# The streams' attention steps start five chunks later, the memory keys get a pool of their own, and a PSUM pair is allocated first

## The chip, the cores and the metric

One core of a Trainium2 chip runs the kernel. The metric is the device time of one execution in microseconds (us): 1756.99 as the median of three runs (1756.55 to 1760.46). TensorE is called PE below, VectorE DVE, ScalarE ACT, GpSimd POOL; SP is the engine that issues most loads, in order.

## The reference

One layer of an encoder step, for 1024 prompt frames and for 8 running streams of 16 frames each (1152 rows of 1024 values in all), in float32:

```python
h = _rmsnorm(x, ln_mix); u, va, q, k, vb = split(h @ w_in)
a_out = u * (tril(w_s) @ va_c + b_s)                    # spatial gating, chunks of 128
z = (q @ k.T) * 64 ** -0.5                              # 8 heads of 64
log_keep = where(mask, log_sigmoid(-z), 0)
between = cumsum(log_keep, reverse=True) - log_keep
sb_out = where(mask, exp(log_sigmoid(z) + between), 0) @ v
x = x + concat(_rmsnorm(a_out), _rmsnorm(sb_out)) @ w_out
s = (h2 @ w_mq) @ mk.T / 16; x = x + (softmax(s) @ mv) @ w_mo   # 4 heads of 256, 256 memory rows
x = x + (silu(h3 @ w_gate) * (h3 @ w_up)) @ w_down      # width 2816
```

The prompt attends to its own keys; a stream attends to its cached 256 keys and its own 16. For the prompt the memory keys and values are computed from mem_prompt, for the streams they are read from a cache.

## The kernel before

Every float32 product is done as three matmuls of a split operand: `split` (L126, L127) writes the rounded value on ACT and the remainder on DVE, `mm3` (L130 to L132) multiplies. The kernel runs in stages: A, the input projection and spatial gating; B, stick-breaking attention; C, the merge into the residual; D, memory attention; E, output projection and feed-forward; then the down projection and the last norm. The order of instructions on each engine is not that of the code: the framework's scheduler lays it down when the program is built, and the engines then run their own lists in order. A buffer that is used again is waited for by address.

**Stage B.** Each of the 8 heads has 12 chunks (`chunk`), 96 in all. A chunk computes z on PE (L385), two sigmoids on ACT (L411, L398), a running product on DVE (pr, L403), a product on POOL (beta, L405), transposes on PE (L389), a split into ath and atl, and products with the values into av. The tasks are started one per step; `tasks()` counts chunks in `n` and starts stream `b` (`stream`) when `n == S0 + SP * b`, with `SP = 10`, and after the eight streams `stream_tails`. A stream transposes its cached keys (kT, L503), and later sums into oTs (L538, and L557 in the tails). In each step, PE work from `memory()` (the memory keys and values of the prompt, weights called mw) and `merge_a()` (the spatial part of the merge) fills up to `SLOT`. At the end oT_d, the attention output in DRAM, is complete; stage C loads it as `or` (L764).

**Stage D.** For each of four heads, `prompt_head` and `stream_head` run side by side. `stream_head` loads cached keys in four pairs (L858), transposes and splits them (`keys`, tiles kth, ktl), multiplies (L934), takes a softmax, loads the cached values in four pairs (vh, vl, L951), and ends with four transposes (L959), a copy to ot (L961) and a store (L962). Buffers come from stack-like pools; stage D's are, in order, `d_q`, `d_k`, `d_a`, `e_z`, `e_k` (the streams' raw pairs, keys and values) and `e_a` (their softmax and results). Worked out from the tile shapes they reach to 67,584 bytes a partition before `e_k`, to 92,160 with it and to 99,328 with `e_a`.

**Stage E.** After `stL.close()` the next pools lie at the same addresses: `f_h` with ten slots of 9,216 bytes (0 to 92,160), then `f_g` with the gain gffn (to 96,256), then `f_x` with the residual tiles xt, three buffers of 4,096 bytes, of which the first ends at 100,352. `out_in(i)` loads xt (L1029) and the attention output or; `out_mm(i)` multiplies and adds on DVE (L1048). Tile 0 uses two accumulators (acc0) that stage D began; the other tiles use PSUM pairs, two of the eight banks each, which get banks in the order of their first use. `norm` (L148, L141, L142, L150) and `turn_halves` (transposes at L1060) follow.

Of the kernel before, what the change touches and what calls it, by code (L numbers as in the profile page):

```python
# [37 lines left out]
def stream_step(ctx: ExitStack, tc: tile.TileContext, I, O, cst):  # L38
    nc = tc.nc

    def pool(stack, name, bufs=1, **kw):
        return stack.enter_context(tc.tile_pool(name=name, bufs=bufs, reuse_waits="tile", **kw))
# [10 lines left out]
    def nm(s):  # L53
        uid[0] += 1
        return f"{s}_{uid[0]}"
# [5 lines left out]
    def ps(tag, shape):  # L61
        n = next(cur[tag])
        return psum[0].tile(shape, F32, tag=f"bank{n}", name=nm(tag))
# [57 lines left out]
    def split(hi, lo, src, gain=None):  # L121
        if gain is not None:
            nc.scalar.activation(hi, src, AF.Copy, scale=gain)
            nc.vector.scalar_tensor_tensor(out=lo, in0=src, scalar=gain, in1=hi.bitcast(F32), op0=ALU.mult, op1=ALU.subtract)
            return
        nc.scalar.copy(hi, src)  # L126
        nc.vector.tensor_tensor(out=lo, in0=src, in1=hi.bitcast(F32), op=ALU.subtract)  # L127
# [80 lines left out]
    with ExitStack() as st:  # L208
# [47 lines left out]
        for i in range(NT):  # L256
# [11 lines left out]
            kt = [ap.tile([P, 4, P], F32R, tag=f"kt{n}", name=nm("kt")) for n in range(2)]  # L268
# [100 lines left out]
    with ExitStack() as st:  # L369
# [44 lines left out]
        def pair(h, c, got):  # L414

            sh = {}
            spans = [(512, 2 * c), (0, 2 * c)] if c >= 2 else [(0, 2 * c)]
            for part, (s, _) in enumerate(spans):
                for qb in (2 * c, 2 * c + 1):
                    e = (qb + 1) * P if part == 0 else 512  # L420
                    yield chunk(h, c, qb, s, e, part, len(spans) - 1, sh, got)
# [62 lines left out]
        def stream_in(b):  # L484
            if b == B:
                vn = kp.tile([P, 2, 512], F32, tag="vr", name="vn")[:, 0]
                nc.sync.dma_start(vn, v_s)
                return vn
            kr = kp.tile([P, 2, 512], F32, tag="kr", name=nm("kr"))
            nc.sync.dma_start(kr, csk[b].rearrange("(n p) d -> p n d", p=P))  # L490
            vr = kp.tile([P, 2, 512], F32, tag="vr", name=nm("vr"))
            nc.sync.dma_start(vr, csv[b].rearrange("(n p) d -> p n d", p=P))
            return kr, vr
# [46 lines left out]
        def stream_tails(vn):  # L540

            tr = ps("tr", [P, P])
            tp_(tr, tails.rearrange("p b k -> p (b k)"), ident)
            wt = kp.tile([P, 4, PAST + Q], F32, tag="kT", name="wt")[:, :, 0:PAST].rearrange("p c (b w) -> p c b w", b=B)
            for c in range(4):
                nc.vector.tensor_tensor(out=wt[:, c], in0=tr[:, None, c * 32:(c + 1) * 32].broadcast_to([P, B, 2 * Q]),
                                        in1=own[:, :, None].broadcast_to([P, B, 2 * Q]), op=ALU.mult)
            yield
            yield
            for c in range(4):  # L550
                av = ps("tr", [P, B, 2, Q])
                mm(av.rearrange("p b e q -> p (b e q)"), lhsT=vn[:, c * P:(c + 1) * P], rhs=wt[:, c].rearrange("p b w -> p (b w)"),
                   start=True, stop=True)
                for e in range(2):
                    r = slice(e * 64, e * 64 + 64)
                    o = oTs[r, c].rearrange("p (b q) -> p b q", b=B)
                    nc.vector.tensor_tensor(out=o, in0=av[r, :, e], in1=o, op=ALU.add)  # L557
                yield
            nc.sync.dma_start(oT_d[:, NP:TOK].rearrange("(c p) t -> p c t", p=P), oTs)
# [131 lines left out]
                if i + 2 < NT:  # L691
                    ins.append(load(i + 2))

        S0 = 4
        SLOT = 4700
        ZC = 1
        LAG = 2
# [2 lines left out]
        def tasks():  # L700
            sgot[0] = stream_in(0)
            n, b = 0, 0
            for h in range(8):
                if 0 < h < 7:
                    head_in(h + 1)
                for c in range(4):
                    for g in pair(h, c, got):
                        yield g
                        n += 1
                        if n == S0 + SP * b and b <= B:  # L710
                            yield stream(b, sgot) if b < B else stream_tails(sgot[B])
                            b += 1
                        elif b and n == S0 + SP * (b - 1) + LAG + 6 and b <= B:
                            sgot[b] = stream_in(b)
# [32 lines left out]
    with stD:  # L747
# [56 lines left out]
        stL = ctx.enter_context(ExitStack())  # L804
# [3 lines left out]
        zp = pool(stL, "e_z")  # L808
        sk = pool(stL, "e_k", bufs=2)
        sa = pool(stL, "e_a")  # L810
        W = 144
        qm = zp.tile([P, 2, 2, 4 * W], F32R, name="qm")
        pm = zp.tile([P, 2, 2, 4 * W], F32R, name="pm")
        for t in (qm, pm):
# [17 lines left out]
        def split_blocks(t, j, src):  # L832
            v = t[:, j].rearrange("p g (b w) -> p g b w", w=W)
            split(v[:, :, :, 0:Q], v[:, :, :, 64:64 + Q], src.rearrange("p (g b q) -> p g b q", g=2, b=4))

        def flat(t):
            return t.rearrange("p n k -> p (n k)")

        def keys(pl, kr):
            tr = ps("tr", [P, 2, 2, P])  # L840
            for dc in range(2):
                for n in range(2):
                    nc.tensor.transpose(tr[:, dc, n, :], kr[:, n, dc * P:(dc + 1) * P], ident)
            kth = pl.tile([P, 2, 2, P], F32R, tag="kth", name=nm("kth"))
            ktl = pl.tile([P, 2, 2, P], F32R, tag="ktl", name=nm("ktl"))
            split(kth, ktl, tr)
            return kth, ktl
# [7 lines left out]
        def pairs(src, cs):  # L855
            for b in range(0, B, 2):
                r = sk.tile([P, 2, 2, 256], F32, tag="raw", name=nm("raw"))
                nc.sync.dma_start(r, src[b:b + 2, :, cs].rearrange("b (n p) d -> p b n d", p=P))  # L858
                yield b, r[:, 0]
                yield b + 1, r[:, 1]  # L860
# [63 lines left out]
        def stream_head(h, qr):  # L924
            cs = slice(h * 256, (h + 1) * 256)
            for dc in range(2):
                split_blocks(qm, dc, qr[dc][:, NP:TOK])
            ss = ps("ss", [P, 2, 256])
            for b, kr in pairs(cmk, cs):
                kt = keys(sk, kr)  # L930
                g, b4 = divmod(b, 4)
                for dc in range(2):
                    for n in range(2):
                        nc.tensor.matmul(ss[:, g], lhsT=qm[:, dc, g, b4 * P:(b4 + 1) * P], rhs=flat(kt[n][:, dc]),  # L934
                                         start=b4 == 0 and dc == 0 and n == 0, stop=b4 == 3 and dc == 1 and n == 1)
                if b % 4 == 3:
                    yield
            p = softmax(sa, fold(ss, "s"), 64)
            tr = ps("tr", [P, 2, P])
            for n in range(2):  # L940
                for g in range(2):
                    nc.tensor.transpose(tr[:, n, g * 64:(g + 1) * 64], p[lo_, g, n * P:(n + 1) * P], ident[lo_, lo_])
            for n in range(2):
                split_blocks(pm, n, tr[:, n])
            ov = ps("ov", [P, 2, 256])
            for b, vr in pairs(cmv, cs):
                vv = values(sk, vr)
                g, b4 = divmod(b, 4)
                for n in range(2):
                    for m in range(2):  # L950
                        nc.tensor.matmul(ov[:, g], lhsT=pm[:, n, g, b4 * P:(b4 + 1) * P], rhs=vv[m][:, n],  # L951
                                         start=b4 == 0 and n == 0 and m == 0, stop=b4 == 3 and n == 1 and m == 1)
                if b % 4 == 3:
                    yield
            oe = fold(ov, "s")
            tr = ps("tr", [P, 2, P])
            for dc in range(2):
                for g in range(2):
                    nc.tensor.transpose(tr[:, dc, g * 64:(g + 1) * 64], oe[lo_, g, dc * P:(dc + 1) * P], ident[lo_, lo_])  # L959
            ot = sa.tile([P, 2, P], F32, tag="ot", name=nm("ot"))  # L960
            nc.vector.tensor_copy(ot, tr)  # L961
            nc.sync.dma_start(omT_d[4][cs, :].rearrange("(c p) t -> p c t", p=P), ot)  # L962
# [43 lines left out]
    with ExitStack() as stE:  # L1006
# [6 lines left out]
        def slot(shape, name):  # L1013
            return slots.tile(shape, F32R, tag="h", name=name)

        def pair(n):
            return psum[0].tile([P, 2, 512], F32, tag=f"pair{n}", name=nm("pp"))

        b11, b21, b22 = ([slot([P, 4, TH], f"{t}{n}") for n in range(2)] for t in ("b11", "b21", "b22"))
        t1, t2, t3, t4 = (slots.tile([P, 4, TH], F32, tag="h", name=f"t{n}") for n in range(1, 5))  # L1020
        gffn = bcast(pool(stN, "f_g"), I["ln_ffn"].rearrange("l d -> (l d)"), D, "gffn")
# [376 lines left out]
```

## Time and profile before

| what | value |
|---|---|
| median of three runs | 1756.99 us |
| profiled execution, its own time | 1759.56 us |
| its span | 1757.8 us |
| PE busy | 1687.9 us, 96% of the span |
| DVE, ACT, POOL busy | 986.7, 676.2, 430.3 us |
| mean granted PE clock | 0.988 of full speed |
| DMA | 229.51 MB, mean 131 GB/s |

The shares are means over stages with different limits. An engine's idle time counts only where the others wait for it. The profile gives the granted clock as a share of 2.4 GHz; 0.50 is 1.2 GHz. In the profile's rows a start is counted from the span's start, and the bracket at the end of a row is the idle time ahead of it with what ended it.

### The profile page before, as it was taken

How to read it: one execution, taken by the hardware profiler on the slowest of the kernel's cores; microseconds unless marked ns; L12 is line 12 of the kernel's file. 1: busy time of each engine (PE TensorE's matmuls, PEld its weight loads, DVE VectorE, ACT ScalarE, POOL GpSimd, SP SyncE). 2: the span in 40 equal slices, each digit the busy share in tenths (PEclk: the TensorE clock that was granted, in tenths of full speed). 3: DMA queues.
4: the chain of work that ended last, by engine and by line, in shares of the span. 5: the costliest groups of instructions: out<-in, count | busy, mean ns of one | idle time of the engine just before them, and what ended most of it. 6: DMA issues, size and time to landing. Idle time of an engine off the chain costs nothing. (4 is left out here: it accounts for less than half of the span.)

```text
span 1757.8 us, 26293 instructions
## 1 busy us (share of the span) xinstructions
PE 1687.9 (96%) x10039; PEld 1498.9 (85%) x10039; DVE 986.7 (56%) x1481; ACT 676.2 (38%) x1326; POOL 430.3 (24%) x574
## 2 busy tenths in 40 slices
PE   8999998999999899999699999999999999999997
PEld 6889887777777799998577899999999999888886
DVE  5312345889788746545535866555555556444444
ACT  5322224777565436545422423233322333011123
POOL 2101224444343220000011254443443332000002
PEclk9999999999999999999899999999999999999999
DMA  8548235667644624343734122222222227322202
GB/s 272 164 165 267 78 114 172 184 193 227 209 135 133 191 99 139 111 131 110 234 127 122 67 81 88 76 76 76 76 76 76 75 89 247 130 102 102 102 13 96
DMA packets 178254, 229.51 MB, mean 131 GB/s; under 512 B 12177, under 2 KB 125457, under 8 KB 178129
## 3 DMA queue, kind: packets, MB, share of 16 engines
q1 hardware_dynamic: 146432, 163.46, 30.8%
q10 hardware_dynamic: 23504, 35.79, 5.5%
q0 software_dynamic: 8192, 28.58, 4.3%
q8 instruction: 80, 1.31, 0.3%
q14 instruction: 46, 0.37, 0.1%
HBM read 163.43 MB, written 64.36 MB: 130 GB/s over the span
## 5 line engine op out<-in xcount | busy, mean ns | idle before, releaser
L1203 PE MATMUL pp<-b,wg 128*128 128x288 f32 x1584 | 221.4, 296 | 3.5 <-ACT wg L126 2.4
L1203 PEld LDWEIGHTS pp<-b,wg 128*128 128x128 f32 x1584 | 213.5, 188 | 4.4 <-ACT wg L126 2.6
L131 PE MATMUL tr<-wd,hid 128*128 128x512 f32 x396 | 154.6, 391 | 0.0
L132 PE MATMUL tr<-wd,hid 128*128 128x512 f32 x396 | 154.0, 389 | 0.0
L130 PE MATMUL tr<-wd,hid 128*128 128x512 f32 x396 | 151.4, 389 | 0.0
L127 DVE TENSOR_TENSOR wg<-s,wg 128x512 fp32r<-128x512 f32 x88 | 86.9, 989 | 99.0 <-ACT wg L126 85.9
L1339 DVE TENSOR_TENSOR xr<-tr,xr 128x512 f32<-128x512 f32 x108 | 73.2, 688 | 119.9 <-PE tr L132 119.5
L405 POOL TENSOR_TENSOR beta<-beta,pr 128x512 f32<-128x512 f32 (+4 forms) x104 | 95.3, 918 | 144.3 <-DVE pr L403 125.5
L130 PE MATMUL acc<-wh,hah 128*128 128x512 f32 x288 | 114.6, 398 | 0.0
L132 PE MATMUL acc<-wh,hal 128*128 128x512 f32 x288 | 113.5, 394 | 0.0
L131 PE MATMUL acc<-wl,hah 128*128 128x512 f32 x288 | 113.2, 393 | 0.0
L126 ACT CAST hid<-hr 128x576 fp32r<-128x576 f32 x44 | 27.5, 670 | 190.5 <-PE tr L132 176.4
L131 PEld LDWEIGHTS tr<-wd,hid 128*128 128x128 f32 x396 | 74.3, 188 | 16.8 <-DVE wd L127 1.5
L126 ACT CAST wg<-s 128x512 fp32r<-128x512 f32 x88 | 54.2, 619 | 87.9 <-DVE g L1187 44.3
L130 PEld LDWEIGHTS tr<-wd,hid 128*128 128x128 f32 x396 | 74.3, 188 | 15.9
L132 PEld LDWEIGHTS tr<-wd,hid 128*128 128x128 f32 x396 | 74.3, 188 | 15.2
L126 ACT CAST wg<-raw 128x512 fp32r<-128x512 f32 x66 | 40.5, 622 | 118.2 <-PE pp L1203 46.7
L1049 POOL DMA_DIRECT2D x_d<-xt x9 | 5.6, 624 | 320.6 <-DVE xt L1048 320.6
L127 DVE TENSOR_TENSOR wl<-raw,wh 128x1024 fp32r<-128x1024 f32 x36 | 44.6, 1247 | 48.9 <-ACT wh L126 48.0
L1351 POOL TENSOR_SCALAR sm<-sm 128x1 f32<-128x1 f32 x9 | 7.1, 792 | 252.8 <-ACT junk L1344 252.8
L1115 POOL TENSOR_TENSOR s<-raw 128x512 f32<-128x512 f32 x22 | 28.9, 1313 | 158.5 <-DMA raw<-in_w_ffn_up_dram 77.8
L130 PE MATMUL acc<-hdh,wh 128*128 128x384 f32 x192 | 66.3, 345 | 0.0
(294 smaller groups left out, 4535.5 us busy)
## 6 DMA issues: line engine op xcount, KB each, us to landing
hr<-hid_d SPq DMA_DIRECT2D x44, 288.0 KB, 5.0
raw<-in_w_ffn_up_dram SPq DMA_DIRECT2D x24, 512.0 KB, 4.1
hid_d<-g ACTq DMA_DIRECT2D x42, 288.0 KB, 2.1
raw<-in_w_ffn_gate_dram SPq DMA_DIRECT2D x23, 512.0 KB, 3.9
raw<-in_w_ffn_down_dram SPq DMA_DIRECT2D x22, 512.0 KB, 4.6
raw<-in_w_in_dram SPq DMA_DIRECT2D x20, 512.0 KB, 5.0
x_d<-xt POOLq DMA_DIRECT2D x18, 512.0 KB, 3.1
raw<-in_cache_mem_k_dram SPq DMA_DIRECT2D x16, 512.0 KB, 4.5
```

The costliest lines, as they stand in the source:

```text
L126: nc.scalar.copy(hi, src)
L127: nc.vector.tensor_tensor(out=lo, in0=src, in1=hi.bitcast(F32), op=ALU.subtract)
L130: nc.tensor.matmul(out, lhsT=lh, rhs=rh, start=first, stop=False)
L131: nc.tensor.matmul(out, lhsT=lh, rhs=rl, start=False, stop=False)
L132: nc.tensor.matmul(out, lhsT=ll, rhs=rh, start=False, stop=last)
L405: nc.gpsimd.tensor_tensor(out=beta[:, :w], in0=beta[:, :w], in1=pr[:, 1:w + 1], op=ALU.mult)
L1049: nc.gpsimd.dma_start(x2_d[i * P:(i + 1) * P, :], xt)
L1115: nc.gpsimd.tensor_tensor(out=s[n], in0=x, in1=y, op=op)
L1203: nc.tensor.matmul(acc[:, h], lhsT=hl[:, a, c], rhs=b[:, c, h * TN:(h + 1) * TN], start=c == 0 and k == 0, stop=c == 3 and k == 2)
L1339: nc.vector.tensor_tensor(out=xr[i][:, hs], in0=pd, in1=xr[i][:, hs], op=ALU.add)
L1351: nc.gpsimd.tensor_scalar(out=tot, in0=ss[:, 0:1], scalar1=ss[:, 1:2], scalar2=EPS, op0=ALU.add, op1=ALU.add)
```

## The change

Three edits. `S0` goes from 4 to 9, so every stream and the tails start five chunks later. The keys of `stream_head` get their own pool `e_kk`, opened behind `e_a`: `e_k` then ends at 83,968 bytes, `e_a` lies from there to 91,136, and the keys from 91,136 to 99,328, under gffn and the first xt. And `pair(0)` is allocated ahead of all others, which gives pair 0 the first two banks (acc0's), pair 1 the next two, pair 2 the two after; before, pair 1 had the first two, pair 2 the next, pair 0 the third. No computation is added or taken away.

```diff
-        S0 = 4
+        S0 = 9
         SLOT = 4700
...
         sk = pool(stL, "e_k", bufs=2)
         sa = pool(stL, "e_a")
+        skk = pool(stL, "e_kk", bufs=2)
...
             for b, kr in pairs(cmk, cs):
-                kt = keys(sk, kr)
+                kt = keys(skk, kr)
...
+        pair(0)
         b11, b21, b22 = ([slot([P, 4, TH], f"{t}{n}") for n in range(2)] for t in ("b11", "b21", "b22"))
```

In the rows below, a tile's name carries a number that differs between the two programs, and behind the edits the lines of the changed program are numbered one to two higher. The first place is SP at the end of stage D's last head: raw are cached values of the last head, or the attention output of tiles 1 to 4, ot the last result of the streams, xt the residual tiles. Before:

```order
L858 DMA raw_8977<-in_cache_mem_v_dram 128x4x256
L974 DMA or_9347<-omT_d_84 128x6x128
L974 DMA or_9347<-omT_d_84 128x2x128
L962 DMA omT_d_86<-ot_9016 128x2x128
L136 DMA gffn<-in_ln_ffn_dram 128x1024
L1029 DMA xt_9065<-x_d 128x1024
L1029 DMA xt_9070<-x_d 128x1024
L1029 DMA xt_9096<-x_d 128x1024
```

and now:

```order
L975 DMA or_9077<-omT_d_82 128x6x128
L136 DMA gffn<-in_ln_ffn_dram 128x1024
L859 DMA raw_8962<-in_cache_mem_v_dram 128x4x256
L1031 DMA xt_9070<-x_d 128x1024
L1031 DMA xt_9075<-x_d 128x1024
L975 DMA or_9077<-omT_d_82 128x2x128
L1031 DMA xt_9101<-x_d 128x1024
L975 DMA or_9103<-omT_d_83 128x6x128
L975 DMA or_9103<-omT_d_83 128x2x128
L859 DMA raw_8980<-in_cache_mem_v_dram 128x4x256
```

Before, all of gffn and xt stand behind the store of ot; now they stand ahead of the last load of values.

The second place is DVE at the start of stage B (mw are remainders of memory weights, atl remainders of transposed chunks, kT the first stream's keys). Before:

```order
L127 TENSOR_TENSOR mw_2380<-raw_2365,mw_2379 128x512 x2
L403 SCALAR_TENSOR_TENSOR pr_2421<-z_2422,zero_69 128x384
L127 TENSOR_TENSOR atl_2459<-tr_2460,ath_2458 128x128
L503 COPY kT_2478<-tr_2512 128x4x128
L403 SCALAR_TENSOR_TENSOR pr_2448<-z_2449,zero_69 128x512
L127 TENSOR_TENSOR mw_2390<-raw_2385,mw_2389 128x512 x2
L127 TENSOR_TENSOR mw_2432<-raw_2393,mw_2431 128x512 x2
L127 TENSOR_TENSOR atl_2459<-tr_2491,ath_2458 128x2x128
L127 TENSOR_TENSOR mw_2469<-raw_2435,mw_2468 128x512 x2
```

and now:

```order
L403 SCALAR_TENSOR_TENSOR pr_2421<-z_2422,zero_69 128x384
L127 TENSOR_TENSOR mw_2380<-raw_2365,mw_2379 128x512 x2
L127 TENSOR_TENSOR atl_2459<-tr_2460,ath_2458 128x128
L403 SCALAR_TENSOR_TENSOR pr_2448<-z_2449,zero_69 128x512
L127 TENSOR_TENSOR atl_2459<-tr_2489,ath_2458 128x2x128
L403 SCALAR_TENSOR_TENSOR pr_2479<-z_2480,zero_69 128x128
L127 TENSOR_TENSOR mw_2390<-raw_2385,mw_2389 128x512 x2
L127 TENSOR_TENSOR mw_2432<-raw_2393,mw_2431 128x512 x2
L433 TENSOR_TENSOR z_2506<-z_2506,csb 128x128
```

The second atl of the first pair (128x2x128) stood behind four weight splits; it now stands ahead of them, and no kT is left here.

The third place is the end of stage B: on DVE, wl is a weight of stage D, sq and ol belong to stage C, oTs to the streams' tails. Before:

```order
L127 TENSOR_TENSOR atl_5633<-tr_5634,ath_5632 128x4x128
L771 TENSOR_REDUCE sq_1147_5790<-sq_5788 128x128
L403 SCALAR_TENSOR_TENSOR pr_5622<-z_5623,zero_69 128x512
L127 TENSOR_TENSOR ol_5802<-or_5799,oh_5801 128x512
L127 TENSOR_TENSOR wl_6427<-raw_6424,wh_6426 128x1024
L127 TENSOR_TENSOR atl_5633<-tr_5660,ath_5632 128x4x128
L403 SCALAR_TENSOR_TENSOR pr_5651<-z_5652,pr_5590,zero_69 128x512
```

and now:

```order
L127 TENSOR_TENSOR atl_5624<-tr_5625,ath_5623 128x4x128
L557 TENSOR_TENSOR oTs<-tr_5637,oTs 64x128 x2
L403 SCALAR_TENSOR_TENSOR pr_5613<-z_5614,zero_69 128x512
L127 TENSOR_TENSOR atl_5624<-tr_5655,ath_5623 128x4x128
L403 SCALAR_TENSOR_TENSOR pr_5646<-z_5647,pr_5585,zero_69 128x512
L127 TENSOR_TENSOR wl_6430<-raw_6427,wh_6429 128x1024
L127 TENSOR_TENSOR atl_5680<-tr_5681,ath_5679 128x3x128
```

The atl of 5633 before, of 5624 now, stood behind the reduction, ol and wl, and now stands ahead of wl and behind two sums into oTs. On SP the store of oTs moves with them; before:

```order
L465 DMA oT_d<-oe_5452 64x256
L559 DMA oT_d<-oTs 128x4x128
L465 DMA oT_d<-oe_5543 64x256
L764 DMA or_5782<-oT_d 128x4x128
L764 DMA or_5799<-oT_d 128x4x128
```

and now:

```order
L465 DMA oT_d<-oe_5445 64x256
L465 DMA oT_d<-oe_5503 64x256
L465 DMA oT_d<-oe_5567 64x256
L559 DMA oT_d<-oTs 128x4x128
L764 DMA or_5782<-oT_d 128x4x128
L764 DMA or_5799<-oT_d 128x4x128
```

The loads of or, which stood behind the oe of one later chunk pair, now stand behind two and the store of oTs.

## Rows read from the trace of the kernel before

**Rows 1.** Windows by stage: length, busy of PE, PEld, DVE, ACT, POOL, clock, DMA.

```profile
550.00:562.00 12.00, 8.32 (x49) 6.83 (x48) 11.97 (x16) 9.22 (x17) 6.15 (x6) 0.94 0.39 111
...
872.00:882.00 10.00, 0.39 (x2) 0.34 (x2) 1.71 (x3) 0.36 (x1) 0.09 (x1) 0.50 0.61 222
```

**Rows 2.** Timeline, end of stage D: start, length, engine, line, operation, tiles, idle before.

```profile
871.37 0.69 PE L959 MATMUL tr<-csb,s 64*128 64x64 f32 x4 [1.39 <-DVE s L921]
...
872.54 0.36 SPq L962 DMA_DIRECT2D omT_d<-ot  x1
...
874.38 11.98 SPq L1029 DMA_DIRECT2D xt<-x_d  x4
880.32 1.29 DVE L1048 TENSOR_TENSOR xt<-acc,xt 128x512 f32<-128x512 f32 x2 [7.81 <-DMA xt<-x_d]
...
881.66 0.79 PE L130 MATMUL pp<-wh,oh 128*128 128x512 f32 x1 [9.61 <-DVE xt L1048]
...
883.80 1.28 DVE L150 SCALAR_TENSOR_TENSOR xs<-xt,sm,gffn 128x1024 f32<-128x1024 f32 x1 [2.19 <-POOL sm L142]
...
888.49 0.60 PEld L1060 LDWEIGHTS pp<-csb,xs 128*128 128x128 f32 x4
```

**Rows 3.** Timeline, the last head's keys and values.

```profile
848.65 0.28 PE L934 MATMUL ss<-ktl,qm 128*128 128x256 f32 x1
...
851.13 0.37 SPq L858 DMA_DIRECT2D raw<-in_cache_mem_v_dram  x1
...
859.68 0.95 DVE L127 TENSOR_TENSOR ol<-or,oh 128x768 fp32r<-128x768 f32 x1
...
861.95 0.37 SPq L858 DMA_DIRECT2D raw<-in_cache_mem_v_dram  x1
...
862.57 1.30 DVE L127 TENSOR_TENSOR vl<-raw,vh 128x512 fp32r<-128x512 f32 x2
...
867.39 0.38 PE L951 MATMUL ov<-vh,pm 128*128 128x256 f32 x1 [2.26 <-ACT vh L126]
```

**Rows 4.** DMA issues, 845 to 885: KB each, median us to landing.

```profile
raw<-in_cache_mem_v_dram SPq DMA_DIRECT2D x3, 512.0 KB, 5.3
xt<-x_d SPq DMA_DIRECT2D x3, 512.0 KB, 6.7
```

**Rows 5.** Windows of 4 us around the hole, columns as in rows 1.

```profile
868.00:872.00 4.00, 2.50 (x11) 2.07 (x11) 1.34 (x3) 0.58 (x1) 0.00 (x0) 0.50 0.11 37
...
880.00:884.00 4.00, 2.33 (x6) 1.85 (x7) 1.49 (x3) 1.15 (x2) 1.41 (x3) 0.50 0.53 211
884.00:888.00 4.00, 4.00 (x17) 3.25 (x16) 1.08 (x1) 0.00 (x0) 0.00 (x0) 0.91 0.31 77
```

**Rows 6.** Waits of PE, stage B: us in total, times, longest.

```profile
PE tr L389 <- DMA kr<-in_cache_sb_k_dram: 0.7, 1, 0.7
```

**Rows 7.** Timeline, start of stage B.

```profile
304.73 3.95 DVE L127 TENSOR_TENSOR mw<-raw,mw 128x512 fp32r<-128x512 f32 x4
...
309.16 0.52 PE L389 MATMUL tr<-csb,beta 128*128 128x128 f32 x3 [2.66 <-DVE atl L127]
```

**Rows 8.** Timeline, end of stage B.

```profile
546.02 0.93 SPq L764 DMA_DIRECT2D or<-oT_d  x2
...
556.20 2.13 DVE L127 TENSOR_TENSOR wl<-raw,wh 128x1024 fp32r<-128x1024 f32 x1
...
558.99 0.38 PE L385 MATMUL av<-atl,vhl 128*128 128x256 f32 x1 [2.78 <-DVE atl L127]
...
562.18 0.78 PE L130 MATMUL acc<-mw,oh 128*128 128x512 f32 x1
...
564.17 1.21 DVE L127 TENSOR_TENSOR wl<-raw,wh 128x1024 fp32r<-128x1024 f32 x1
```

**Rows 9.** DVE by lines, stage B: busy us, mean ns of one.

```profile
L557 DVE TENSOR_TENSOR oTs<-tr,oTs 64x128 f32<-64x128 f32 x8 | 2.3, 286 | 0.2
```

**Rows 10.** A window of 2 us, end of stage B.

```profile
562.00:564.00 2.00, 2.00 (x7) 1.65 (x6) 2.00 (x4) 0.58 (x1) 1.09 (x1) 0.50 0.67 269
```

## The prediction

> **What bounds the kernel now.** I read the windows by stage first, then the timeline where TensorE (PE) stands still, then the issues of the DMA queue on SP, last the waits in the stick-breaking stage. PE is the bound nearly everywhere, so only time in which PE stands still, or runs at its lower clock, can be won. Two places hold most of what this change touches. Between the memory attention and the output projection PE works 0.39 us of ten [rows 1]. In the stick-breaking stage it loses many short waits, and in its last twelve microseconds VectorE (DVE) is busy 11.97 of 12.00 while PE has 8.32 [rows 1].
>
> The reader is to see the hole step by step [rows 2]. PE ends the streams' last transposes, begun at 871.37. SP, which issues in order, stores their result at 872.54; only behind it come the broadcast of the gain (gffn) and, from 874.38, the residual tile xt, whose buffer lies over what that store reads. DVE adds xt to the accumulators at 880.32, in two rows of together 1.29 us, and releases PE at 881.66: the first matmul row shows 9.61 us of waiting on that add, since its PSUM pair is the banks that the add reads. PE could have begun at 872.06, behind the transposes' 0.69.
>
> **The keys under the residual buffer.** With the keys' tiles in a pool of their own behind the others, gffn and the first xt lie over keys instead of over the last softmax and the last result. PE's last read of a key is the matmul at 848.65 [rows 3]. In the new SP order gffn stands ahead of the third load of memory values, and three residual tiles stand ahead of the fourth. That third load went out at 851.13 [rows 3], when its buffer came free, so xt can be asked for near 852. With the median landing of 6.7 [rows 4] it is there by about 858.5. The two adds stand in DVE's new order where the split of a 768-wide ol stood at 859.68 [rows 3]; they take 1.29 against its 0.95, and the 256-wide ol moves behind them. So both accumulators are read, and xt summed, by about 861, ten microseconds before PE comes to the output projection. The hole of 9.61 goes.
>
> What is late next is the streams' own tail, which ends at 872.06. Its last pair of values was issued at 861.95 [rows 3]. Ahead of the third pair's vl rows, DVE now has the normalisation xs, 1.28 long, 2.19 after the add because of ScalarE's square and POOL's power [rows 2]: from 861 it ends at 861 + 2.19 + 1.28 = 864.5, or some later, since in the new order two casts stand ahead of the square on ScalarE. So the third pair's vl, which began at 862.57 and took 1.30 [rows 3], end near 866 to 867, up to 3 us later. The fourth pair's come behind them and the ol splits of 1024 columns, about 1.3 us by the 0.95 for 768, so near 868; PE began with that pair at 867.39 [rows 3]. I take 1.0 us of delay for the transposes. Term: -9.6 + 1.0 = **-8.6 us**. Bounds: the fourth load could land a whole landing late, 5.3 [rows 4], which leaves -4.3; or there is no delay and the clock stays up, below.
>
> The granted clock is half, 1.2 GHz, from 868 to 884 and 0.91 in the next row [rows 5]. PE had stood still before that: it waited 2.26 us on the fourth pair's first cast [rows 3]. The work done at the lower clock is 2.50 us in one row and 2.33 in the other [rows 5]; half of that, 2.4 us, is what it costs. The wait on the cast stays, and PE will still start again after a pause, so I count nothing for the clock; the 2.4 us is kept for the range.
>
> **The pairs laid anew.** The pair of the first full tile moves from the banks of the early accumulators to banks idle since the softmax. But the add that held those banks now ends at about 861, so the new layout hides behind the new load: **0 us**. Alone it would be worth something: PE could run 24 matmuls from 872 (17 in 4 us [rows 5], so under 6 us) and then wait for the transposes' input, ready at 883.80 + 1.28 = 885.1, against 888.49 in the trace [rows 2], so some 3 us.
>
> **The streams five steps later.** Same instructions, same sum of work; only waits can change. PE's wait for the first cached keys is 0.7 us [rows 6]. The largest early wait is at 309.16, 2.66 us for an atl that DVE ran behind four weight splits of 3.95 [rows 7]. In the new order that atl stands ahead of those splits and the copies are gone from there; what PE then needs is only the first two of the splits, and it has the next chunk's products to do until then. Term: **-2.7 us**; bounds 0 to -3.4 (with the cached keys' wait).
>
> At the end, PE waits 2.78 us at 558.99 for an atl behind a 128x1024 weight split of 2.13 [rows 8]; the new order puts that atl ahead of the split, the reduction and the 512-wide ol. Against it, the tails' eight sums into oTs, 286 ns each [rows 9], come into the stretch where DVE is full: 8 x 0.286 = 2.3. Term: -2.8 + 2.3 = **-0.5 us**. Bounds: with the wait and also the half clock gone (the row at 562, wholly at half [rows 10], costs 1.0; over the next three windows like it some 3 us) -5.8; with the wait back behind other rows and the sums on top, +5.
>
> The shared-port rule speaks against this part. The split took 2.13 us at 556.20 and 1.21 at 564.17 [rows 8]. The Trainium skill, SBUF — State Buffer, "SBUF: two separate sides", says that a DVE instruction with two SBUF inputs and a GpSimd instruction that reads SBUF block each other for a whole instruction. The two durations agree. By it the split, which now stands directly ahead of another atl and beside the last chunks' products on POOL, would hold that atl 0.9 us longer, and the end term would be +0.4. Only the size of the sum would change.
>
> The remaining short waits of the stage are dealt anew; their sum can move either way by about 3 us, and I take 0.
>
> **Sum.** -8.6 + 0 - 2.7 - 0.5 = -11.8 us, against the profiled execution's 1759.56 (its span of 1757.8 and 1.8 around it): 1747.8. The profiled execution lies 2.6 above the median of the timed runs, 1756.99; the same difference from the median gives **1745.2 us**.
>
> **Rivals.**
> 1. The clock stays up too, in the hole or at the end of the stick-breaking stage: -2.4 and up to -3 more, about 1740. For it: less standing still at both places. Against: the 2.3 us wait that precedes the fall stays. Chance 0.20.
> 2. The last load of values becomes late: three residual tiles and one attention tile, 512 KB each, stand ahead of it on SP's queue. For it: a 512 KB load of values took 5.3 us to land there, a residual tile 6.7 [rows 4]. Against: it waits for its buffer until 862 in any case, 10 us after the others are issued. Price one landing: -4.3 - 3.2 = -7.5, 1749.5. The Trainium skill, DMA: Bandwidth & Descriptors, "Queues, rings and completion order", says that each engine takes one ring's descriptors in order, which is this case if the others are still under way. Chance 0.15.
> 3. The hole goes but the stick-breaking stage deals worse: end term +5, start 0, so -3.6, 1753.4. For it: DVE has no idle time left there. Chance 0.13.
> 4. The gain is given back where weights for the feed-forward stage stream in, half of it: about 1751. Against: all its loads stand behind the residual tiles on the same queue, so they come earlier too. Chance 0.05.
> 5. Slower: the loads of the attention output (tile `or`) now stand on SP behind the store of oTs, which waits for the tails' last sum; before, they were issued at 546.02 and PE first multiplied them at 562.18 [rows 8], so 16 us of cover. In DVE's new order that last sum stands 19 rows behind the sum that released them before; at the 0.75 us of a row in that stretch (16 in 11.97 [rows 1]) that is 14 us. If they come over 16 us later PE stands still; with the sums' 2.3, a wait of 5 or more, and the opening of the merge (48 matmuls, 11 us at 17 in 4 us [rows 5]) at the lower clock, some 18 us are lost, and -8.6 becomes +7 to +9: about 1765. It decides once the first cast of `or` begins after 562. Chance 0.05.
>
> That the change does not do what it says is excluded by the order: xt stands ahead of the values there.
>
> **Chances and range.** The forecast (1742 to 1749) has 0.42. Within 0.2%, 3.5 us, no change can be told apart. Slower by more: rival 5, 0.05. Same: half of rival 3 and a little of 4, 0.08. Faster: the rest, 0.87. The range 1736.5 to 1752.5 takes in the clock's gain below and rivals 2 and 4 above.
>
> **What would show it.** Right: SP issues xt near 852; DVE's first add near 860; PE's first matmul of the output projection within 1 us of the last transposes, near 873 less what the streams won; no wait on xt there; the early 2.66 gone. The pair matters not at all once xt is early. Wrong: the fourth values' first matmul comes after 869 in the old count; PE waits over 3 us for the first `or`; or the way from the output projection to the steady feed-forward products gets longer.

## The result, and the profile after

The changed kernel takes 1748.08 us (median of 4 runs, 1746.41 to 1749.42), the kernel before beside it 1758.13: a ratio of 0.995, with a 95% interval of 0.9933 to 0.9968. Timed again on another chip (below) it was 0.9943 (0.9926 to 0.9959). So it is 9 to 10 us faster. The forecast was 1745.2, in a range of 1736.5 to 1752.5; the direction and the range held, the gain was forecast some 2 to 3 us too large. The profiled execution takes 1747.44, its span 1745.7.

The timeline of the changed kernel around the former hole, which answers to [rows 2, 3]: start, duration, engine, line, operation, and in brackets the idle time ahead and what ended it.

```profile
846.92 0.34 SPq L136 DMA_DIRECT2D gffn<-in_ln_ffn_dram  x1
...
849.15 0.37 SPq L859 DMA_DIRECT2D raw<-in_cache_mem_v_dram  x1
849.61 0.93 SPq L1031 DMA_DIRECT2D xt<-x_d  x2
...
856.78 1.29 DVE L1050 TENSOR_TENSOR xt<-acc,xt 128x512 f32<-128x512 f32 x2 [0.84 <-DMA xt<-x_d]
...
861.71 1.28 DVE L150 SCALAR_TENSOR_TENSOR xs<-xt,sm,gffn 128x1024 f32<-128x1024 f32 x1 [1.50 <-POOL sm L142]
...
863.65 0.39 PE L952 MATMUL ov<-vl,pm 128*128 128x256 f32 x1 [2.00 <-DVE vl L127]
...
865.47 0.38 PE L952 MATMUL ov<-vh,pm 128*128 128x256 f32 x1 [0.59 <-ACT vh L126]
...
869.26 0.69 PE L960 MATMUL tr<-csb,s 64*128 64x64 f32 x4 [1.39 <-DVE s L922]
869.88 0.79 PE L130 MATMUL pp<-wh,oh 128*128 128x512 f32 x1
...
877.06 0.60 PE L1062 MATMUL pp<-csb,xs 128*128 128x128 f32 x4
```

The residual tile goes out behind the third load of values, not behind the store of the streams' result; DVE adds it at 856.78, 13 us before PE begins the output projection; and the first matmul of the output projection follows the last transposes with no bracket at all, where [rows 2] have 9.61.

The granted clock behind it, in 4 us windows (columns as in [rows 5]; the third figure from the end is the clock):

```profile
864.00:868.00 4.00, 2.94 (x15) 2.17 (x13) 2.69 (x5) 1.23 (x3) 0.00 (x0) 0.80 0.99 315
868.00:872.00 4.00, 2.74 (x9) 2.24 (x10) 1.11 (x2) 0.49 (x1) 0.00 (x0) 0.50 0.88 228
872.00:876.00 4.00, 4.00 (x16) 3.21 (x16) 0.00 (x0) 0.00 (x0) 0.00 (x0) 0.84 0.01 2
```

It still falls to 1.2 GHz, as PE stands still before the values' products; the stretch is shorter than in [rows 5], but PE works through it, so little is won by that.

The waits of PE in the stick-breaking stage (us in total, times, longest):

```profile
PE tr L389 <- DMA ar<-a_d: 3.4, 1, 3.4
...
PE acc L130 <- DVE xt L785: 2.5, 1, 2.5
PE av L385 <- ACT ath L126: 2.4, 4, 1.6
PE tr L389 <- DVE atl L127: 2.1, 6, 0.4
PE av L385 <- DVE atl L127: 1.8, 3, 1.0
```

The waits of 2.66 and 2.78 for atl [rows 7, 8] are gone; the longest for atl is 1.0 us. In the place of the first stands a shorter one, for an ath:

```profile
311.43 0.39 PE L385 MATMUL av<-ath,vhl 128*128 128x256 f32 x1 [1.57 <-ACT ath L126]
```

The first line of the list is new: ar is the spatial part of a tile for the merge, a load that no step of the forecast named.

### The profile page after: what moved, and what is told of

Read it like the earlier page. It is cut to its first block, busy times and chain, and to the rows that moved or that the text cites. A ratio compares the mean times of both kernels' runs of the same rounds, so it can differ in the third digit from the quotient of the medians.

```text
span 1745.7 us, 26300 instructions
## 1 busy us (share of the span) xinstructions
PE 1689.2 (97%) x10039; PEld 1497.6 (86%) x10039; DVE 981.8 (56%) x1481; ACT 674.4 (39%) x1326; POOL 433.4 (25%) x574
## 4 chain that ended last, share of the span: by engine, by line
PE 76%; DMA 6%; DVE 6%; issue 6%; ACT 3%; POOL 1%; SPq 0%; POOLq 0%; ACTq 0%; DVEq 0%
PE pp L1205 27%; PE acc L130 5%; PE acc L132 5%; PE acc L131 5%; PE tr L131 5%; PE tr L132 5%; PE tr L130 5%; PE acc L385 3%; PE tr L389 2%; PE z L385 2%; PE pp L130 2%; PE pp L131 2%; PE pp L132 1%; PE av L385 1%; DMA or<-oT_d 1%
## 5 line engine op out<-in xcount | busy, mean ns | idle before, releaser
L127 DVE TENSOR_TENSOR wg<-s,wg 128x512 fp32r<-128x512 f32 x88 | 79.4, 904 | 96.7 <-ACT wg L126 83.6
L127 DVE TENSOR_TENSOR wg<-raw,wg 128x512 fp32r<-128x512 f32 x66 | 61.5, 932 | 12.6 <-ACT wg L126 12.6
```

## The experiments

Twelve more runs were made, each with one profile; e5 and e9 are the two kernels unchanged, and all but e5 were timed. Because stages vary from execution to execution, the profiles are compared by stage. This table is worked out from the timelines. Merge: start of the first add of the merge (DVE, `xt<-acc,sm,xt`), that is, how late the stick-breaking stage ends. Tail: from PE's last product with a key (`ss<-`) to the last transpose of the streams' result. Way: from that product to the first transpose of the normalised tile. Rest: from there to the end.

```
                          merge    tail    way    rest
before                   574.17   23.09  40.08   869.0
e5 before again          576.77   21.92  38.68   869.6
e1 streams only          572.98   21.16  37.75   869.4
e3 pair only             576.73   21.20  34.59   871.1
e10 pair again           572.70   22.00  36.24   871.3
e2 keys only             573.96   23.53  31.40   868.1
e4 streams, keys         572.65   22.95  31.52   869.8
changed                  573.23   22.95  30.37   868.6
e9 changed again         572.06   24.50  31.78   868.5
e6 third raw buffer      573.43   23.76  30.84   868.4
e7 S0 = 7                570.43   22.05  30.18   869.6
e12 S0 = 8               572.68   23.10  30.57   868.6
e8 S0 = 11               577.13   22.50  30.85   869.7
e11 S0 = 7, third raw    569.18   23.43  30.51   868.8
```

**e1, the streams alone.**

```
-        S0 = 4
+        S0 = 9
```

> Only the streams come later (S0 = 9 instead of 4); the keys stay in their old pool and the pairs keep their banks. Theory (terms add up): the forecast's term of -3.2 us, that is 1755.0 from a median of 1758.1; the trace of the changed kernel, which is 1.98 us ahead when the third load of memory values is issued, would make it -2.0, 1756.1. The 9.6 us wait for the residual tile must still be there, at a place 2 to 3 us earlier. Rival 1, the streams do most of the change: -8 or more, 1750 or less. Rival 2, the streams' start only changes which waits are seen, 0 us: 1758.

Measured: 1755.38 against 1755.77, ratio 0.9993 (0.9984 to 1.0002): -1.2 us, between -2.8 and +0.4. The wait for the residual tile is still there, 5.2 us earlier than in [rows 2] and not 2 to 3, with a new wait in the stage ahead:

```profile
412.46 0.30 PE L389 MATMUL tr<-csb,ar 128*128 128x128 f32 x1 [2.36 <-DMA ar<-a_d]
...
876.49 0.79 PE L130 MATMUL pp<-wh,oh 128*128 128x512 f32 x1 [8.37 <-DVE xt L1048]
```

Rival 1 falls. The time alone can't separate -2 from 0. In the table merge is 572.87 on the mean of the five executions with S0 = 9 and 574.87 on that of the five with S0 = 4, so -2.0; but the five lie between 572.06 and 573.43, and between 572.70 and 576.77, so they overlap, and rival 2 (0 us) is made unlikely, not excluded. The streams added to the keys (e4 against e2, on one chip) give -0.7 us between the medians, 1749.08 and 1749.74.

**e2, the keys alone.**

```
+        skk = pool(stL, "e_kk", bufs=2)
...
-                kt = keys(sk, kr)
+                kt = keys(skk, kr)
```

> Only the keys' tiles move into a pool of their own behind the others. Theory: the residual tile is issued near 852 and the 9.6 us wait is gone; forecast -8.6, and -10 by what the changed kernel's trace gained behind 850 us (11.8 at the first output-projection matmul less 2.0): 1748 to 1749.5. Stick-breaking waits (2.66 us at 309, 2.78 at 559, end at half clock) stay as before. Rival (the banks of the pair close the hole): without the new pair PE still waits for the add, and not more than 3 us are gained, 1755 or more.

Measured: 1749.74, ratio 0.9966 (0.9953 to 0.9978): -6.0 us, between -8.3 and -3.9. The issue of the residual tile, and PE's first matmul of the output projection, which has no bracket:

```profile
850.93 0.93 SPq L1030 DMA_DIRECT2D xt<-x_d  x2
...
871.83 0.79 PE L130 MATMUL pp<-wh,oh 128*128 128x512 f32 x1
```

The rival falls: the hole closes without new banks. The way is 31.40, and that is 8.7 less than in the profile of before, the 8.6 of the forecast. But it is only 7.4 less than the mean of the three executions that still have the hole, 38.84 (before, e5, e1), taken with e4's 31.52. The expectation of -10 had been read from two single profiles and was too large.

**e3 and e10, the pair alone,** timed twice.

```
+        pair(0)
         b11, b21, b22 = ([slot([P, 4, TH], f"{t}{n}") for n in range(2)] for t in ("b11", "b21", "b22"))
```

> Only the pair of the first full tile is asked for before the other tiles, so it gets other banks; the residual tile stays late. Theory: PE begins the output projection of the next tile right behind the last transposes, near 872, runs 24 matmuls and then waits for the transposes' input until 885: about -3 us, 1755, between 0 (if the matmuls stand behind those transposes) and -4. Rival (the banks close the hole): -8 or more, 1750 or less. After the 24 matmuls a wait of some 6 us must show before the transposes of the normalised tile.

> The kernel before with the new banks for the pair alone, timed a second time. The profile of the first run had the hole 3.1 us shorter than the mean of three executions that keep the old banks, yet its time was +1.4 us (-1.2 to +3.9). Theory (the time was scatter of the stages ahead, whose instructions are those of before): now -1 to -3 us. Rival (something behind the hole takes it back every time): again 0 or slower.

Measured: ratios 1.0008 (0.9993 to 1.0022) and 0.9991 (0.9981 to 1.0000): +1.4 and -1.6 us. The way is 3.4 us shorter (35.4 against 38.84), as the forecast had it for the pair alone, but 1.9 of it are given back in the rest (871.2 against 869.3). PE's timeline in e10, and its windows (columns as above):

```profile
882.00 1.11 PE L1061 MATMUL pp<-csb,xs 128*128 128x128 f32 x4 [5.66 <-DVE xs L150]
```

```profile
872.00:876.00 4.00, 4.00 (x16) 3.19 (x14) 0.00 (x0) 0.00 (x0) 0.00 (x0) 0.81 0.85 261
876.00:880.00 4.00, 0.34 (x2) 0.00 (x0) 1.29 (x2) 1.15 (x2) 0.84 (x2) 1.00 0.55 225
880.00:884.00 4.00, 2.00 (x7) 1.81 (x8) 2.12 (x3) 0.59 (x1) 0.57 (x1) 0.55 0.56 176
884.00:888.00 4.00, 4.00 (x12) 3.09 (x12) 0.46 (x1) 0.00 (x0) 0.00 (x0) 0.60 0.20 79
```

PE does its 24 matmuls, then stops for the normalised tile, and the clock, back at 1.00, falls a second time while PE works. The 6.00 us of work in the last two rows, at 0.55 and 0.60, would be 2.00 x 0.55 + 4.00 x 0.60 = 3.5 at full clock, so this costs about 2.5; in [rows 5] the clock is at 0.91 in the row at 884, ahead of the transposes at 888.73. In e3, whose second stop is 4.64 us, the same reckoning gives 1.2 (2.47 us of work at 0.64 and 4.00 at 0.93), with as much given back, so the second fall isn't shown to be all of it. Each theory was half right: something behind takes over half of the gain back, and e3's profile comes from a late stage ahead (merge 576.73, in e10 572.70, with the same instructions). That e3's timed runs were slow for that reason is not shown; the two intervals, -1.2 to +3.9 and -3.3 to 0.0, overlap.

**e4, all but the pair** (e1 and e2 together).

> The whole change without the new banks for the pair (the streams later and the keys' pool). Theory: the add that reads the old banks begins near 857 and ends near 858, twelve microseconds before PE needs them, so the pair is worth 0: 1748.1, within 1 us of the changed kernel. Rival (the pair matters beside the early residual tile): 3 us or more slower than the changed kernel, 1751 or more, with a wait of PE at the first matmul of the output projection.

Measured: 1749.08, ratio 0.9957 (0.9943 to 0.9971): -7.5 us. There is no wait at the first matmul of the output projection: it starts 0.24 behind the start of the last transpose, as in the changed kernel. The rival falls: nothing waits for the banks. That the pair is worth nothing beside the early tile is not shown: the ways differ by 0.7 us (31.46 on the mean of e2 and e4 without it, 30.75 on that of the five with it and two raw buffers), and single ways with it lie 1.6 apart; the ratio is 1.2 to 2.5 us behind the two of the changed kernel, with intervals that overlap.

**e5, the kernel before once more.**

> The kernel before, unchanged, once more under the profiler. Question: is the hole of the profiled execution (40.1 us from the last product with the keys at 848.65 to the first transpose of the normalised tile at 888.73) the usual one, and how far do two executions of one program lie apart in the stick-breaking stage? Theory (the hole hangs on the landing of the residual tile, 5.9 us from issue to the add there): with landings of 4.7 to 5.2, as in the two runs that still have the hole, 37.5 to 39 us; the stick-breaking stage up to 5 us later than in the first profile, as in two runs of the same instructions. Rival (the first profile is typical): both within 0.5 us of it.

Measured: span 1757.8, as in the first profile, by other stages: merge 2.6 us later, the stretch from there to the last product with a key 1.8 shorter, way 1.4 shorter, rest 0.6 longer. The landing of the residual tile is 4.5 us (issued 873.98, added 878.45) against 5.9 [rows 2]. The early wait in e5, and the window around it in before and in e5:

```profile
309.89 0.87 PE L389 MATMUL tr<-csb,beta 128*128 128x128 f32 x3 [3.16 <-DVE atl L127]
```

```profile
308.00:316.00 8.00, 6.84 (x42) 5.28 (x44) 6.99 (x15) 6.40 (x15) 1.31 (x4) 1.00 0.70 218
```

```profile
308.00:316.00 8.00, 6.11 (x22) 5.37 (x23) 6.13 (x13) 3.29 (x9) 0.80 (x3) 0.57 0.64 206
```

In before the clock stayed at 1.00 through the 2.66 us wait [rows 7]; in e5 it fell to 0.57 behind one of 3.16, and only 22 matmuls ran in place of 42. Two other executions with S0 = 4 had this wait at 2.63 (e3) and 2.62 us (e10), and there the clock fell too, to 0.57 and 0.79 in this window. So the first profile had an unlucky hole, the longest of three, and luck with the clock at the start of the stick-breaking stage; as a whole its stage was the middle one of five (merge 574.17).

**e6, a third buffer for the streams' raw pairs.**

```
-                r = sk.tile([P, 2, 2, 256], F32, tag="raw", name=nm("raw"))
+                r = sk.tile([P, 2, 2, 256], F32, tag="raw", bufs=3, name=nm("raw"))
```

and the streams' p, t and ot in one buffer, so that the addresses behind stay.

> The changed kernel with a third buffer for the streams' raw pairs; p, t and ot of the streams share one buffer so that the gain and the residual tile still lie under the keys only. All four value loads then stand ahead of the gain on SP, and DVE splits the third pair of values ahead of the normalisation. Theory (what is late in the hole is the streams' tail, held by the buffer of the fourth values and by the third pair's split behind the 1.28 us normalisation): the waits of 2.00 and 0.59 before the values' products go, the last transposes come 2 to 3 us earlier against the last product with the keys than the 22.6 us of the changed kernel, and the time falls by 1.5 to 4 us, the 4 if the clock also stays up: 1744 to 1746.5 where the changed kernel has 1748. Rival (the chain of the streams' own softmax sets the end, or the residual tile's transfer is pushed back by the values' and the wait returns): no gain, within 1 us, or a wait on xt.

Measured: 1746.93, ratio 0.9942 (0.9930 to 0.9953), which is not separable from the changed kernel's. The tail is not shorter, 23.76 and in e11 23.43. PE's timeline:

```profile
854.23 0.50 PE L130 MATMUL acc<-wh,oh 128*128 128x512 f32 x1 [2.16 <-ACT wh L126]
...
864.32 0.38 PE L952 MATMUL ov<-vh,pm 128*128 128x256 f32 x1 [0.36 <-ACT vh L126]
866.32 0.58 PE L952 MATMUL ov<-vl,pm 128*128 128x256 f32 x1 [1.61 <-DVE vl L127]
```

The wait of 2.00 ahead of the third pair is gone, but 2.16 for a weight split now stands ahead of the first pair and 1.61 ahead of the last. A miss: with a third buffer the tail is no shorter. The edit also puts p, t and ot into one buffer, and what that costs was not run apart.

**e7, e12, e8: S0 = 7, 8 and 11,** all else as in the changed kernel.

> The changed kernel with S0 = 7 instead of 9. Theory A (the later the streams, the more of the early wait and of the full last stretch is gone): between S0 = 4 and S0 = 9, so 0 to +1.5 us against the changed kernel. Theory B (each step deals the short waits anew, without a trend): anywhere between -3 and +3 us. The stage behind stick-breaking is the same in both.

> The changed kernel with S0 = 8. If there is a trend from 4 over 7 to 9 with a turn before 11, between the times of 7 and 9: 0 to -1.5 us against the changed kernel. If each step deals the waits anew, anywhere within 3 us of it on either side.

> The changed kernel with S0 = 11 instead of 9. Theory A (a trend): 0 to -1 us against the changed kernel, until the tails' sums hold up the loads of the attention output. Theory B (no trend, a new deal): -3 to +3. Theory C (the cover of those loads is used up: they hang on the tails' last sum, which stands two steps later): +3 or more, with PE waiting at the first product of the merge.

Measured: ratios 0.9940 (0.9926 to 0.9955), 0.9947 (0.9930 to 0.9963) and 0.9977 (0.9964 to 0.9989): -10.5, -9.3 and -4.0 us. Theory A falls: merge is at 570.43, 572.68 and 577.13 for 7, 8 and 11, against 572.06 to 573.43 for 9, so later is not better. The times of 7, 8 and 9 can't be told apart. S0 = 11 is slower than 9 by 4.8 to 6.0 us between the ratios, more than theory B allows and what theory C allows. Its loads of the attention output, and PE's first product of the merge:

```profile
566.08 1.15 SPq L764 DMA_DIRECT2D or<-oT_d  x2
...
571.59 0.79 PE L130 MATMUL acc<-mw,oh 128*128 128x512 f32 x1 [0.68 <-ACT oh L126]
```

The loads go out ten microseconds later than in the changed kernel (556.05). PE's wait there is only 0.68, but in e8 that product stands behind the last product of the last chunk (570.49), where in the changed kernel it comes at 562.15, among those products, which end at 567.64. So in e8 no product of the merge fills PE's waits between the last chunks, one of them 1.49 for an atl, and the clock is 0.81 from 550 to 577. The trace leans to theory C, the cover of those loads; no kernel changed it alone. What 7 has over 9 is seen in the loads and PE's wait around 410, first the changed kernel, then e7:

```profile
402.28 0.38 SPq L492 DMA_DIRECT2D vr<-in_cache_sb_v_dram  x1
404.17 0.38 SPq L490 DMA_DIRECT2D kr<-in_cache_sb_k_dram  x1
406.55 0.34 SPq L641 DMA_DIRECT2D ar<-a_d  x1
...
411.73 0.30 PE L389 MATMUL tr<-csb,ar 128*128 128x128 f32 x1 [3.36 <-DMA ar<-a_d]
```

```profile
397.92 0.39 SPq L492 DMA_DIRECT2D vr<-in_cache_sb_v_dram  x1
...
404.95 0.33 SPq L641 DMA_DIRECT2D ar<-a_d  x1
...
410.90 0.63 PE L389 MATMUL tr<-csb,ar 128*128 128x128 f32 x4
...
411.39 0.43 SPq L490 DMA_DIRECT2D kr<-in_cache_sb_k_dram  x1
```

With S0 = 9 a stream's cached keys and values go out on SP directly ahead of the first tile of the merge; with 7 the keys go out behind it, and PE doesn't wait for it. But the keys are not what held that load last. ar takes the buffer of mo, a result of `memory()` (both have the tag "mo" in one pool), and SP waited with it for the store of mo; SP's own waits in the changed kernel, from 404.6 to 406.9:

```profile
SPq L641 <- DMA out_dram<-mo: 1.9, 1, 1.9
```

The load then took 5.0 us to land, and 5.8 in e7, so it was not slower than there. PE was ready for it at 408.37, 6.8 us after the copy into mo at 401.54; in e7 at 410.90, 10.4 us after the copy at 400.47. All five executions with S0 = 9 have that wait (2.4 to 3.4 us), each with a granted clock of 0.91 from 400 to 420; of the five with S0 = 4 one is under 1.00 there. That ar's transposes now stand too close behind the copy into mo is read from the traces; no kernel changed it alone.

**e9, the changed kernel again, and e11,** S0 = 7 with e6's buffer, beside it on one chip.

> The changed kernel, unchanged, timed beside the next three on one chip. From its first timing (ratio 0.995, 0.9933 to 0.9968) and from its parts (keys -6.0, streams -1.2): 0.9945 to 0.9965. If the parts add up without the pair, -7.2 us; if the pair adds what the profiles of the hole show (9.85 against 8.68 us), -8.4.

> The changed kernel with S0 = 7 and the third raw buffer together. If both gains are real (S0 = 7 about -1.5 us against 9, the third buffer -0.6 in the profile of the hole): 1 to 3 us faster than the changed kernel on this chip, ratio 0.992 to 0.994. If both were scatter: the same as the changed kernel, within 1 us.

Measured: e9 1747.70, 0.9943 (0.9926 to 0.9959); e11 1746.55, 0.9933 (0.9917 to 0.9949). e9, at -10.0, lies beyond the larger of the two sums expected of it (-8.4), though the interval, -13.0 to -7.2, holds both. e11 is the fastest version run, with the earliest merge of all, 569.18, but its interval overlaps e9's: that it gains on the changed kernel is not shown.

## Why the prediction was right, and where it was off

**The keys.** Right in the mechanism: tile xt was issued at 849.61, and the add began at 856.78; with the 2.0 us that the streams were ahead, that is 851.6 and 858.8 in the old count, forecast 852 and 860. The tail's delay, forecast at 1.0, is 1.0: 23.1 on the mean of the seven profiles with the keys moved and two raw buffers, 22.1 on that of before, e5 and e1. That it fits so well is in part luck: between the profile of before and that of the changed kernel the tail is not longer (23.09 and 22.95), and single tails in a group lie 1.9 to 2.5 apart. Off was the size. The 9.61 of [rows 2] was taken as the hole, and it is the longest of three (8.12 in e5, 8.37 in e1), since the tile's landing varies. The term of -8.6 is -7.4 by the mean of profiles and -6.0 (-8.3 to -3.9) in time.

**The clock.** Counted at nothing, and nothing is right for the hole: the 24 matmuls up to the first transposes take 7.18 us in the changed kernel and 7.07 before. Rival 1, a gain from it, did not come there; at the end of the stick-breaking stage it came in part, as shown below for the streams.

**The pair.** Forecast 0 beside the early tile; nothing waits for its banks (e4), but the runs leave open whether it is worth a microsecond or two. Alone the forecast of 3 us holds for the way but not for the time: what is given back behind it, with a second fall of the clock, was not in the working.

**The streams.** Forecast -3.2, measured -2.0 by merge, in groups that overlap, and -1.2 (-2.8 to +0.4) in time. The step that failed is the one on the remaining short waits: "their sum can move either way by about 3 us, and I take 0". The early wait, 2.6 to 3.2 us in all five executions with S0 = 4, did go, but one of 0.3 to 1.6 for an ath stands in its place, and the clock behind it is won only in part: from 308 to 316 it is under 1.00 in three of the five executions with S0 = 9 (0.72 to 0.84), in four of the five with S0 = 4 (0.57 to 0.79). And a wait of up to 3.36 for ar came, with a low clock of its own. At the end the wait of 2.78, which is 1.9 in the other four with S0 = 4, went, and the clock rose, in before and in the changed kernel:

```profile
562.00:575.00 13.00, 11.74 (x58) 9.89 (x56) 8.85 (x16) 3.42 (x6) 3.77 (x7) 0.80 0.48 158
```

```profile
562.00:575.00 13.00, 10.35 (x58) 8.47 (x59) 11.15 (x18) 5.85 (x11) 3.18 (x8) 1.00 0.84 274
```

The other four with S0 = 4 have 0.87 to 1.00 there, the five with S0 = 9 0.97 to 1.00. From the means, 0.88 and 0.99, over some 11.3 us of work, that is worth about 1.2 us, an estimate. The 0.9 us longer hold of an atl behind the 128x1024 split did not come: the split took 1.20 us at 558.65, and it is POOL's beta, begun beside it at 558.88, that took 1.92 where the ones around it take 1.09 and 1.10. The wait for ar could have been looked for: ar's tile has the tag of mo, so its load can't go out before mo's store is done.

**The other rivals.** The fourth values' first matmul came at 865.47, 867.5 in the old count and not after 869, so rival 2 did not decide. The stage of rival 3 dealt better, not worse; with S0 = 11 the whole change is worth only -4.0 us, so rival 3 was near. The rest behind the way is the same within 0.4 us (869.0 with the change, 869.3 before), so nothing was given back there (rival 4). In both orders the loads of the attention output stand behind the store of oTs; what the change moves is that store, from 541.36 to 555.62. The loads went out at 556.05, ten microseconds later than in [rows 8], and PE did not wait for them: it first multiplied them at 562.15, so 6 us of the 16 of cover were left (rival 5).

**The sum.** -2.0 for the streams, -8.1 for the way (30.75 against 38.84), -0.3 for the rest: -10.4, against -8.8 and -10.0 timed. The stretch from merge to the last product with a key is left out of it: it is 272.5 to 275.9 us in these profiles, and 0.3 longer on the mean of the five with the change than on that of before, e5 and e1.

## What to carry over

A buffer's address is part of its schedule: what was last read at an address decides when the next tenant's load may be issued, and moving the earliest-dead tiles there can close a hole with no instruction changed. The new wait for ar hangs on a buffer too, mo's. When a wait goes, ask what starts again behind it: work brought forward that then stops a second time (the pair alone) gives back what it won. And price a term from several executions where its size hangs on a DMA landing or on the clock; one profile gave 9.61 for what was 8.1 to 8.4 in two others.

## What the runs showed of the hardware

The same instructions ended the stick-breaking stage at times up to 4.1 us apart (merge 572.70 to 576.77 with S0 = 4). Part of this scatter is the granted clock: behind the same early wait it stayed at 1.00 in one execution (2.66 us) and fell in two others (2.63 us, 0.57 from 308 to 316; 2.62 us, 0.79), and behind a wait of 2.36 it fell in e1 (0.74 from 412 to 416). So here the length of a stop does not by itself tell whether the clock falls. The kernel before took 1755.77, 1756.45 and 1758.51 us (medians) beside the three groups of experiments, so only ratios within a group were used for the times.
